# Second MLP stage of a transformer block: operand halves split over two slabs, combinations of the last chunk one per slab, x1 read back for two tiles

## The chip, the cores and the metric

One core of a Trainium2 chip runs the whole kernel in one launch. Times are device microseconds. The engines work side by side, each through its own queue in order: TensorE (PE, matrix products; PEld is its weight load), VectorE (DVE), ScalarE (ACT), GpSimd (POOL) and SyncE (SP), which here only issues DMAs. GpSimd and ScalarE issue DMAs too. An instruction whose input isn't there holds up everything behind it on its engine. The median of three runs before the change is 2258.95 us (2256.57 to 2261.75).

## The reference, cut to what matters

The block computes attention and retention, adds the result to x (this sum is called x1 here), and ends with an MLP. For 512 tokens of 2048 features in float32:

```python
x = x + rms_norm(mix, norm_mix_post[l])           # x1
h = rms_norm(x, norm_mlp_pre[l])
u = jnp.square(jax.nn.relu(h @ w_up[l]))          # first MLP stage: 512 x 8192
x = x + rms_norm(u @ w_down[l], norm_mlp_post[l]) # second MLP stage
```

`rms_norm(x, g)` is `x * rsqrt(mean(x*x) + eps) * g`, the mean over the 2048 features of a token. The change lies in the last line alone.

## The kernel before, in words

**Products.** Every float32 operand is split in two: a high half (a cast on ScalarE, `whi` for weights and `Hh` for the others) and a low half (the rest, a subtraction on VectorE, `wlo` and `Hl`). A product takes three matmuls: high by high, high by low, low by high (lines 154 to 156, helper `mm3`).

**Seven products instead of eight.** Both MLP stages cut their matrices in 2 x 2 blocks and form seven products of sums of blocks, after Winograd's form of Strassen's scheme. The products are numbered 0 to 6 and run in the order 0, 1, 2, 5, 4, 3, 6. Sums of weight blocks are made as the slabs come: by VectorE (line 949), for product 3 by an accumulating DMA from GpSimd (line 916). Sums of u blocks come ready-made from DRAM (`ud`).

**The second stage** (function `down`) goes through 8 chunks of the inner dimension (`c`), in each through two column halves of 1024 (`nb`), in each through the seven products: 112 phases. A phase is one product for two token tiles, two slabs of weights, 24 matmuls of 128x512. Per slab VectorE makes one `wlo` (line 929), and for products 2, 4 and 6 first a weight sum (line 949), which ScalarE's cast (line 953) needs. `Feed` holds three slabs in work.

After each phase `dn_done` adds the product to the sum `E[nb][p]` (line 1315; chunk 0 copies, line 1312). It is called at the next phase's first slab. In the last chunk it also forms the four result blocks from the seven sums: blocks 11 and 12 (token tiles 0 and 1; columns 0 to 511 and 512 to 1023 of the half), 21 and 22 (tiles 2 and 3). Before the change these combinations (lines 1319, 1323, 1324, 1327, 1335 to 1337) follow each other at once; `finished` squares a block on ScalarE with a running sum (line 1294), and `out_tile` makes the tile's root (line 1300, and a power on GpSimd in `inv_root`, line 161), scales by root and gain on VectorE (line 1304) and adds the result to `out` by an accumulating DMA from GpSimd (line 1305). `out` has held x1 since the start of the MLP. Tiles 2 and 3 wait for the very last product.

**The u operand.** `u_operand` fetches a product's u block from DRAM to a raw buffer through SyncE (line 1282) and splits it three slabs later: `split` issues the cast on ScalarE (line 143) and right behind it the subtraction on VectorE (line 144). Chunk 0 has two raw buffers (in `xh`), the others four (in rows 1 and 3 of `Y`); a fetch waits until the buffer's last subtraction is done. Weight slabs are fetched through SyncE as well (line 923).

**Order of the work.** The order of each engine's queue is the order in which this program emits instructions: per slab first `feed.slab()`, then `dn_done`, then what `later` has due (`later.add(n, work)` runs `work` n slabs on), then the matmuls.

Of the kernel before, what the change touches and what calls it, by code (L numbers as in the profile page):

```python
# [10 lines left out]
F32 = mybir.dt.float32  # L11
F32R = mybir.dt.float32r
AF = mybir.ActivationFunctionType
ALU = mybir.AluOpType
AX = mybir.AxisListType.X

P = 128
S = 512
NT = S // P
DM = 2048  # L20
# [92 lines left out]
def block_kernel(ctx: ExitStack, tc: tile.TileContext, x, norm_mix_pre, w_in, cmp_pe_k, cmp_w1_k, cmp_b1_k,  # L113
                 cmp_w2_k, cmp_pe_v, cmp_w1_v, cmp_b1_v, cmp_w2_v, t5_bias, w_out, norm_mix_post, norm_mlp_pre,
                 w_up, w_down, norm_mlp_post, c_rot, c_dec, c_hot, c_misc, out):
    nc = tc.nc
    x, out = x[0], out[0]
# [23 lines left out]
    def split(hi, lo, src):  # L141

        nc.scalar.copy(hi, src)  # L143
        nc.vector.tensor_sub(lo, src, hi.bitcast(F32))  # L144

    def rows_of(t):
        return slice(t * P, (t + 1) * P)

    def wide(g, c0, n):

        return bass.AP(tensor=g.tensor, offset=g.offset + c0, ap=[[0, P], [1, n]])

    def mm3(ps, ah, al, bh, bl, first, last):
        nc.tensor.matmul(ps, ah, bh, start=first, stop=False)  # L154
        nc.tensor.matmul(ps, ah, bl, start=False, stop=False)  # L155
        nc.tensor.matmul(ps, al, bh, start=False, stop=last)  # L156

    def inv_root(dst, ss, tmp, n, scale):

        nc.vector.tensor_scalar(tmp, ss, scale, EPS, op0=ALU.mult, op1=ALU.add)  # L160
        nc.gpsimd.tensor_tensor(dst, tmp, mhalf[:, :n], op=ALU.pow)
# [220 lines left out]
    for q in (2, 3):  # L382
        c = slice(q * 512, (q + 1) * 512)
# [19 lines left out]
    for n in range(4 * NT):  # L403
        t, q = n // 4, n % 4
# [142 lines left out]
    scale = DK ** -0.5  # L547
# [254 lines left out]
    fp = ctx.enter_context(tc.tile_pool(name="ffn", bufs=1, reuse_waits="tile"))  # L802
    Y = fp.tile([P, NT, DM], F32, name="Y")
    st = [fp.tile([P, 16], F32, name=f"st{t}") for t in range(NT)]
# [164 lines left out]
    class Later:  # L969
# [5 lines left out]
        def add(self, slabs, work):  # L975
            self.todo.append((self.at + slabs, work))
# [8 lines left out]
    later = Later()  # L985
# [119 lines left out]
    NCH = 8  # L1105
# [170 lines left out]
    ua = [tuple(H[:, c:c + SL] for H in (Hhf, Hlf)) for c in range(16, 16 + 7 * SL, SL)]  # L1276
    stage, stage0 = Ring(*(Y[:, t, c:c + SL] for t in (1, 3) for c in (0, SL))), Ring(xh[:, :SL], xh[:, SL:])

    def u_operand(c, p):

        r = (stage if c else stage0).take()
        nc.sync.dma_start(r.rearrange("p (b n) -> p b n", b=2), ud[p, 2 * c:2 * c + 2].rearrange("b p n -> p b n"))
        later.add(3, lambda: split(ua[p][0], ua[p][1], r))

    g4 = low[:, 4096:6144]

    def cols(nb, j):
        return slice(nb * 1024 + j * 512, nb * 1024 + (j + 1) * 512)

    def finished(nb, t0, j, v):  # L1290

        for t in (0, 1):
            jk = fp.tile([P, S], F32, name="jk", tag="jk")
            nc.scalar.activation(jk, v[:, t, :], AF.Square, accum_out=st[t0 + t][:, 2 * nb + j:2 * nb + j + 1])

    def out_tile(t, half):

        s = st[t]
        if half:
            nc.vector.reduce_sum(s[:, 5:6], s[:, 0:4], axis=AX)  # L1300
            inv_root(s[:, 7:8], s[:, 5:6], s[:, 6:7], 1, 1.0 / DM)
        for j in range(2):
            v = res[half, t // 2, j][:, t % 2, :]
            nc.vector.scalar_tensor_tensor(v, v, s[:, 7:8], g4[:, cols(half, j)], op0=ALU.mult, op1=ALU.mult)
            nc.gpsimd.dma_start(out[rows_of(t), cols(half, j)], v, accum_op=ALU.add)

    res = {}

    def dn_done(c, nb, p, ps):
        e = E[nb]  # L1310
        if c == 0:
            nc.scalar.copy(e[p], ps)
            return
        if c < NCH - 1 or p != 6:
            nc.vector.tensor_add(e[p], ps, e[p])  # L1315
        if c < NCH - 1:
            return
        if p == 1:
            nc.vector.tensor_add(e[1], e[1], e[0])
            res[nb, 0, 0] = e[1]  # L1320
            later.add(1, lambda: finished(nb, 0, 0, e[1]))
        elif p == 4:
            nc.vector.tensor_add(e[4], e[4], e[0])
            nc.vector.tensor_sub(e[2], e[2], e[4])

            def more():
                nc.vector.tensor_add(e[5], e[5], e[2])
                res[nb, 0, 1] = e[5]
                finished(nb, 0, 1, e[5])
                if nb:  # L1330
                    for n, (t, half) in enumerate(((0, 1), (0, 0), (1, 1), (1, 0))):
                        later.add(1 + n // 2, lambda t=t, half=half: out_tile(t, half))
            later.add(1, more)
        elif p == 3:
            nc.vector.tensor_add(e[4], e[4], e[3])
            nc.vector.tensor_add(e[6], e[6], e[4])
            nc.vector.tensor_sub(e[3], e[2], e[3])
            res[nb, 1, 1] = e[3]
            finished(nb, 2, 1, e[3])
        elif p == 6:  # L1340
            res[nb, 1, 0] = e[6]
            for t in (0, 1):
                nc.vector.tensor_add(e[6][:, t], ps[:, t], e[6][:, t])
                if nb:
                    jk = fp.tile([P, S], F32, name="jk", tag="jk")
                    nc.scalar.activation(jk, e[6][:, t], AF.Square, accum_out=st[2 + t][:, 2:3])
                    out_tile(2 + t, 1)
                    out_tile(2 + t, 0)
            if not nb:
                finished(nb, 2, 0, e[6])  # L1350

    sets2 = []

    def down():
        for i, ((_, c, nb), p, _) in enumerate(phases[nup:]):
            ps = pools[(nup + i) % len(pools)].tile([P, 2, S], F32, name="prod")
            final = nup + i == len(phases) - 1
            at = i % 7
            slabs = []
            for s in range(2):  # L1360
                slabs.append([v.rearrange("p (k n) -> p k n", k=2) for v in feed.slab()])
                if s == 0 and sets2:
                    dn_done(*sets2.pop())
                if s == 0 and i == 0:
                    up_done(*sets.pop())
                later.step()
                if s == 0 and i == 7:
                    nc.sync.dma_start(g4, wide(norm_mlp_post, 0, DM))
                if s == 1 and nb == 1 and c + 1 < NCH and at:
                    u_operand(c + 1, ORDER[at - 1])  # L1370
                if s == 1 and nb == 0 and at in ((0,) if c else (0, 1, 2)):
                    u_operand(c, 6 if c else ORDER[4 + at])
                if final and s == 0:
                    continue
                for t in range(2):
                    for s2 in range(2) if final else (s,):
                        for kk in range(2):
                            k = 2 * s2 + kk
                            uh, ul = (u.rearrange("p (k n) -> p k n", k=4) for u in ua[p])
                            mm3(ps[:, t, :], uh[:, k, rows_of(t)], ul[:, k, rows_of(t)], slabs[s2][0][:, kk, :],  # L1380
                                slabs[s2][1][:, kk, :], k == 0, k == 3)
            sets2.append((c, nb, p, ps))
        dn_done(*sets2.pop())


    for n, _ in enumerate(up(last, nup, pools, XA)):
        if n % 4 == 2 and n < 16:
            u_operand(0, ORDER[n // 4])
    sctx.close()
    accp = ctx.enter_context(tc.tile_pool(name="acc", bufs=1, reuse_waits="tile"))  # L1390
    Et = [accp.tile([P, SL], F32, name=f"acc{i}") for i in range(12)] + [xh[:, :SL], xh[:, SL:]]
    E = [[Et[nb * 7 + p].rearrange("p (t n) -> p t n", t=2) for p in range(7)] for nb in range(2)]
    down()
    while later.todo:
        later.step()
# [23 lines left out]
```

## Time and profile before

| | us |
|---|---|
| median of three runs | 2258.95 |
| profiled execution | 2263.74 |
| its span | 2261.9 |
| TensorE busy | 2175.6 (96%) |
| VectorE busy | 1563.7 (69%) |
| ScalarE busy | 986.9 (44%) |
| GpSimd busy | 129.1 (6%) |

The second stage's matmuls begin near 1595 us and end near 2233 us; the span ends at 2261.9 us. Busy shares are means over stages with different limits, so the stages are read one by one. Matmuls overlap in the trace: one lasts 0.39 us but starts 0.227 us after the one before it. A VectorE instruction on 1024 columns lasts 1.22 us, and the next starts 1.13 us after it. In a timeline a number of idle time in brackets, with an arrow, tells how long the engine stood and for whom.

### The profile page before, as it was taken

Reading aid. Unit: us, or ns where it says so; the run is one execution under the profiler, and the core shown is the slowest. Engines: PE = TensorE matmul, PEld = TensorE weight load, DVE = VectorE, ACT = ScalarE, POOL = GpSimd, SP = SyncE. Lnnn points to the kernel's source line nnn. Section 1 sums busy time; section 2 is a strip of 40 time slices with the busy share of each in tenths; the row PEclk is TensorE's granted clock in tenths of the full one; section 3 lists DMA queues with packets and bytes.
Section 4 is the critical chain, followed back from the end, with each engine's and each line's share of the span. In section 5 each row is a group of like instructions: output and inputs, shape, how many; then the busy total and the mean of one; then the engine's idle time right before and its main releaser. Section 6 shows DMA issues by size and latency. Waiting matters only on the chain.

```text
span 2261.9 us, 31774 instructions
## 1 busy us (share of the span) xinstructions
PE 2175.6 (96%) x12787; PEld 1919.0 (85%) x12787; DVE 1563.7 (69%) x1868; ACT 986.9 (44%) x1432; POOL 129.1 (6%) x147
## 2 busy tenths in 40 slices
PE   8999999999999999889999999999899999999994
PEld 7888878878787999889999999999778888888873
DVE  6223556554656623587777878787778998899897
ACT  5213343342232323564554555555654444444442
POOL 0000000000000000100000000000000000000002
PEclk9999999999999999999999999999999999999997
DMA  6543224322324334675876767666665656566655
GB/s 191 140 118 91 79 73 95 90 75 87 89 70 145 95 106 127 205 213 169 223 204 178 203 168 206 168 208 187 202 208 160 212 159 214 152 205 165 192 144 83
DMA packets 251989, 344.76 MB, mean 152 GB/s; under 512 B 14107, under 2 KB 163947, under 8 KB 251201
## 3 DMA queue, kind: packets, MB, share of 16 engines
q1 hardware_dynamic: 212000, 288.23, 39.4%
q0 software_dynamic: 29744, 42.96, 12.0%
q10 hardware_dynamic: 10098, 11.55, 1.5%
q8 instruction: 100, 1.64, 0.3%
q14 instruction: 47, 0.39, 0.1%
HBM read 300.95 MB, written 41.75 MB: 152 GB/s over the span
## 4 chain that ended last, share of the span: by engine, by line
PE 77%; DVE 12%; DMA 4%; ACT 3%; issue 3%; POOL 1%; SPq 0%; ACTq 0%; POOLq 0%; DVEq 0%
PE prod L155 13%; PE prod L156 13%; PE prod L154 13%; PE mm L154 11%; PE mm L156 10%; PE mm L155 10%; DVE wlo L929 4%; DMA Y<-in_w_up 2%; DVE Hl L144 2%; PE S L583 2%; ACT whi L953 1%; DVE low L949 1%; DVE Y L949 1%; DVE acc L1315 1%; DMA low<-in_w_up 1%
## 5 line engine op out<-in xcount | busy, mean ns | idle before, releaser
L953 ACT CAST whi<-Y 128x1024 fp32r<-128x1024 f32 x228 | 238.4, 1049 | 305.8 <-DVE Y L949 119.0
L155 PE MATMUL prod<-wlo,Hh 128*128 128x512 f32 x896 | 352.3, 393 | 18.3 <-DVE wlo L929 18.3
L156 PE MATMUL prod<-whi,Hl 128*128 128x512 f32 x896 | 349.0, 390 | 0.0
L154 PE MATMUL prod<-whi,Hh 128*128 128x512 f32 x896 | 348.7, 389 | 0.0
L953 ACT CAST whi<-low 128x1024 fp32r<-128x1024 f32 x214 | 224.3, 1052 | 282.2 <-DVE low L949 105.9
L144 DVE TENSOR_TENSOR wlo<-raw,whi 128x1024 fp32r<-128x1024 f32 (+4 forms) x152 | 168.6, 1113 | 255.9 <-ACT whi L143 255.4
L929 DVE TENSOR_TENSOR wlo<-Y,whi 128x1024 fp32r<-128x1024 f32 x228 | 277.6, 1222 | 61.6 <-ACT whi L953 59.9
L929 DVE TENSOR_TENSOR wlo<-low,whi 128x1024 fp32r<-128x1024 f32 x214 | 260.8, 1222 | 54.4 <-ACT whi L953 52.7
L156 PE MATMUL prod<-Hh,wlo 128*128 128x256 f32 x1024 | 286.2, 279 | 11.2 <-DVE wlo L929 11.2
L154 PE MATMUL prod<-Hh,whi 128*128 128x256 f32 x1024 | 285.7, 279 | 5.1 <-DVE Y L824 5.1
L155 PE MATMUL prod<-Hl,whi 128*128 128x256 f32 x1024 | 284.7, 278 | 0.0
L143 ACT CAST whi<-raw 128x1024 fp32r<-128x1024 f32 (+4 forms) x152 | 145.4, 960 | 302.5 <-PE mm L155 147.9
L154 PE MATMUL mm<-whi,Hh 128*128 128x416 f32 (+4 forms) x704 | 263.3, 374 | 0.5 <-ACT Hh L143 0.4
L156 PE MATMUL mm<-whi,Hl 128*128 128x416 f32 (+4 forms) x704 | 248.6, 353 | 0.6 <-DVE Hl L144 0.5
L155 PE MATMUL mm<-wlo,Hh 128*128 128x416 f32 (+4 forms) x704 | 248.1, 352 | 0.0
L155 PEld LDWEIGHTS prod<-wlo,Hh 128*128 128x128 f32 x896 | 168.1, 188 | 65.5 <-DVE wlo L929 31.0
L156 PE MATMUL prod<-sx,wlo 128*128 128x256 f32 x768 | 215.1, 280 | 8.1 <-DVE wlo L929 8.1
L154 PE MATMUL prod<-sx,whi 128*128 128x256 f32 x768 | 214.7, 280 | 0.5 <-ACT whi L953 0.5
L154 PE MATMUL mm<-Hh,whi 128*128 128x512 f32 x512 | 214.7, 419 | 0.1
L155 PE MATMUL prod<-sx,whi 128*128 128x256 f32 x768 | 214.5, 279 | 0.0
L156 PEld LDWEIGHTS prod<-Hh,wlo 128*128 128x128 f32 x1024 | 194.3, 190 | 13.6 <-DVE wlo L929 13.4
L156 PE MATMUL mm<-Hh,wlo 128*128 128x512 f32 x512 | 200.5, 392 | 0.0
(289 smaller groups left out, 3970.4 us busy)
## 6 DMA issues: line engine op xcount, KB each, us to landing
raw<-in_w_in SPq DMA_DIRECT2D x160, 256.0 KB, 3.1
low<-in_w_up SPq DMA_DIRECT2D x38, 1024.0 KB, 6.2
Y<-in_w_up SPq DMA_DIRECT2D x32, 1024.0 KB, 6.1
low<-in_w_down SPq DMA_DIRECT2D x32, 1024.0 KB, 5.2
Y<-in_w_down SPq DMA_DIRECT2D x32, 1024.0 KB, 5.2
Y<-ud SPq DMA_DIRECT2D x49, 512.0 KB, 8.4
ud<-Y SPq DMA_DIRECT2D x73, 256.0 KB, 4.7
raw<-in_w_out SPq DMA_DIRECT2D x32, 416.0 KB, 3.5
```

What stands on the lines that cost most here:

```text
L143: nc.scalar.copy(hi, src)
L144: nc.vector.tensor_sub(lo, src, hi.bitcast(F32))
L154: nc.tensor.matmul(ps, ah, bh, start=first, stop=False)
L155: nc.tensor.matmul(ps, ah, bl, start=False, stop=False)
L156: nc.tensor.matmul(ps, al, bh, start=False, stop=last)
L583: nc.tensor.matmul(sps[:, :c + L], QT[g][:, h, qs], k, start=True, stop=True)
L929: nc.vector.tensor_sub(lo, src, hi.bitcast(F32))
L949: nc.vector.tensor_add(to, to, by)
L953: nc.scalar.copy(hi, src)
L1315: nc.vector.tensor_add(e[p], ps, e[p])
```

## The change

- The u operand's cast stays three slabs behind its fetch; the subtraction is issued one slab later, four behind.
- In the last chunk the combinations are put into two lists, `vec` and `act`, and `spare()` takes at most one entry from each per slab. The combinations are written as single additions and subtractions, nine per column half instead of seven. The gain is multiplied in on VectorE block by block (`gained`), where it was part of the last scaling before.
- Tiles 0 and 1: ScalarE scales by the root (`out_first`), and GpSimd's accumulating DMA adds to `out` as before.
- Tiles 2 and 3: x1 is read back from `out` into rows 1 and 3 of `Y` during the last chunk's first half; VectorE scales and adds x1 in one instruction (`out_last`), and SyncE writes the result by a plain DMA.
- In the second column half, products 4 and 3 first empty both lists and then do what the next block needs at once.

```diff
--- before.py
+++ after.py
@@ -1280,74 +1280,134 @@
 
         r = (stage if c else stage0).take()
         nc.sync.dma_start(r.rearrange("p (b n) -> p b n", b=2), ud[p, 2 * c:2 * c + 2].rearrange("b p n -> p b n"))
-        later.add(3, lambda: split(ua[p][0], ua[p][1], r))
+        later.add(3, lambda: nc.scalar.copy(ua[p][0], r))
+        later.add(4, lambda: nc.vector.tensor_sub(ua[p][1], r, ua[p][0].bitcast(F32)))
 
     g4 = low[:, 4096:6144]
 
     def cols(nb, j):
         return slice(nb * 1024 + j * 512, nb * 1024 + (j + 1) * 512)
 
-    def finished(nb, t0, j, v):
-
-        for t in (0, 1):
-            jk = fp.tile([P, S], F32, name="jk", tag="jk")
-            nc.scalar.activation(jk, v[:, t, :], AF.Square, accum_out=st[t0 + t][:, 2 * nb + j:2 * nb + j + 1])
-
-    def out_tile(t, half):
-
+
+    vec, act = [], []
+
+    def spare():
+        for todo in (act, vec):
+            if todo:
+                todo.pop(0)()
+
+    res = {}
+
+    def square(nb, q, t, v):
+
+        jk = fp.tile([P, S], F32, name="jk", tag="jk")
+        nc.scalar.activation(jk, v, AF.Square, accum_out=st[t][:, 2 * nb + q % 10 - 1:2 * nb + q % 10])
+
+    def gained(nb, q, v, ts):
+
+        g = g4[:, None, cols(nb, q % 10 - 1)]
+        nc.vector.tensor_tensor(v[:, ts], v[:, ts], g.to_broadcast([P, ts.stop - ts.start, S]), op=ALU.mult)
+
+    def there(nb, q, v):
+
+        res[nb, q] = v
+
+        def squares():
+            for t in (0, 1):
+                square(nb, q, q // 10 * 2 - 2 + t, v[:, t])
+            vec.append(lambda: gained(nb, q, v, slice(0, 2)))
+        act.append(squares)
+
+    def root(t):
         s = st[t]
-        if half:
-            nc.vector.reduce_sum(s[:, 5:6], s[:, 0:4], axis=AX)
-            inv_root(s[:, 7:8], s[:, 5:6], s[:, 6:7], 1, 1.0 / DM)
-        for j in range(2):
-            v = res[half, t // 2, j][:, t % 2, :]
-            nc.vector.scalar_tensor_tensor(v, v, s[:, 7:8], g4[:, cols(half, j)], op0=ALU.mult, op1=ALU.mult)
-            nc.gpsimd.dma_start(out[rows_of(t), cols(half, j)], v, accum_op=ALU.add)
-
-    res = {}
+        nc.vector.reduce_sum(s[:, 5:6], s[:, 0:4], axis=AX)
+        inv_root(s[:, 7:8], s[:, 5:6], s[:, 6:7], 1, 1.0 / DM)
+
+    def quarters(t):
+        for nb in range(2):
+            for j in range(2):
+                yield res[nb, t // 2 * 10 + 11 + j][:, t % 2], cols(nb, j)
+
+    def out_first(t):
+
+        for v, c in quarters(t):
+            nc.scalar.activation(v, v, AF.Copy, scale=st[t][:, 7:8])
+            nc.gpsimd.dma_start(out[rows_of(t), c], v, accum_op=ALU.add)
+
+    x1b = {2: Y[:, 1, :], 3: Y[:, 3, :]}
+
+    def out_last(t):
+
+        for v, c in quarters(t):
+            nc.vector.scalar_tensor_tensor(v, v, st[t][:, 7:8], x1b[t][:, c], op0=ALU.mult, op1=ALU.add)
+            nc.sync.dma_start(out[rows_of(t), c], v)
 
     def dn_done(c, nb, p, ps):
         e = E[nb]
         if c == 0:
             nc.scalar.copy(e[p], ps)
             return
-        if c < NCH - 1 or p != 6:
-            nc.vector.tensor_add(e[p], ps, e[p])
+        if c == NCH - 1 and p == 6 and nb:
+            for t in (0, 1):
+                ts = slice(t, t + 1)
+                nc.vector.tensor_add(e[6][:, t], ps[:, t], e[6][:, t])
+                square(1, 21, 2 + t, e[6][:, t])
+                gained(1, 21, e[6], ts)
+                root(2 + t)
+                out_last(2 + t)
+            return
+        nc.vector.tensor_add(e[p], ps, e[p])
         if c < NCH - 1:
             return
+
+        def op(f, to, by):
+            vec.append(lambda: f(e[to], e[to], e[by]))
+
+        add, sub = nc.vector.tensor_add, nc.vector.tensor_sub
         if p == 1:
-            nc.vector.tensor_add(e[1], e[1], e[0])
-            res[nb, 0, 0] = e[1]
-            later.add(1, lambda: finished(nb, 0, 0, e[1]))
+            op(add, 1, 0)
+            vec.append(lambda: there(nb, 11, e[1]))
+        elif p == 2:
+            op(sub, 2, 0)
+        elif p == 5:
+            op(add, 5, 2)
+            op(add, 6, 0)
+        elif p == 4 and not nb:
+            op(sub, 5, 4)
+            vec.append(lambda: there(nb, 12, e[5]))
+            op(sub, 2, 4)
+            op(add, 6, 4)
         elif p == 4:
-            nc.vector.tensor_add(e[4], e[4], e[0])
-            nc.vector.tensor_sub(e[2], e[2], e[4])
-
-            def more():
-                nc.vector.tensor_add(e[5], e[5], e[2])
-                res[nb, 0, 1] = e[5]
-                finished(nb, 0, 1, e[5])
-                if nb:
-                    for n, (t, half) in enumerate(((0, 1), (0, 0), (1, 1), (1, 0))):
-                        later.add(1 + n // 2, lambda t=t, half=half: out_tile(t, half))
-            later.add(1, more)
+            while vec or act:
+                spare()
+            sub(e[5], e[5], e[4])
+            res[1, 12] = e[5]
+            for t in (0, 1):
+                square(1, 12, t, e[5][:, t])
+            op(sub, 2, 4)
+
+            def roots():
+                gained(1, 12, e[5], slice(0, 2))
+                for t in (0, 1):
+                    root(t)
+                    act.append(lambda t=t: out_first(t))
+            vec.append(roots)
+            op(add, 6, 4)
+        elif p == 3 and not nb:
+            op(sub, 2, 3)
+            vec.append(lambda: there(nb, 22, e[2]))
+            op(add, 6, 3)
         elif p == 3:
-            nc.vector.tensor_add(e[4], e[4], e[3])
-            nc.vector.tensor_add(e[6], e[6], e[4])
-            nc.vector.tensor_sub(e[3], e[2], e[3])
-            res[nb, 1, 1] = e[3]
-            finished(nb, 2, 1, e[3])
+            while vec or act:
+                spare()
+            sub(e[2], e[2], e[3])
+            res[1, 22], res[1, 21] = e[2], e[6]
+            for t in (0, 1):
+                square(1, 22, 2 + t, e[2][:, t])
+            add(e[6], e[6], e[3])
+            gained(1, 22, e[2], slice(0, 2))
         elif p == 6:
-            res[nb, 1, 0] = e[6]
-            for t in (0, 1):
-                nc.vector.tensor_add(e[6][:, t], ps[:, t], e[6][:, t])
-                if nb:
-                    jk = fp.tile([P, S], F32, name="jk", tag="jk")
-                    nc.scalar.activation(jk, e[6][:, t], AF.Square, accum_out=st[2 + t][:, 2:3])
-                    out_tile(2 + t, 1)
-                    out_tile(2 + t, 0)
-            if not nb:
-                finished(nb, 2, 0, e[6])
+            vec.append(lambda: there(nb, 21, e[6]))
 
     sets2 = []
 
@@ -1364,6 +1424,9 @@
                 if s == 0 and i == 0:
                     up_done(*sets.pop())
                 later.step()
+                spare()
+                if c == NCH - 1 and nb == 0 and at in (4, 5) and s:
+                    nc.sync.dma_start(x1b[at - 2], out[rows_of(at - 2), :])
                 if s == 0 and i == 7:
                     nc.sync.dma_start(g4, wide(norm_mlp_post, 0, DM))
                 if s == 1 and nb == 1 and c + 1 < NCH and at:
```

## Rows read from the trace of the kernel before

**Rows 1.** Stretches; from:to, length, busy us (instructions) by engine, granted clock, DMA share, GB/s.
```profile
1740.00:1817.50 77.50, 76.99 (x337) 62.78 (x336) 70.75 (x61) 35.72 (x36) 4.73 (x4) 1.00 0.61 183
2128.00:2205.00 77.00, 72.89 (x315) 58.05 (x314) 73.68 (x65) 38.34 (x49) 4.73 (x4) 1.00 0.52 157
```

**Rows 2.** Waits of TensorE and VectorE, 1595 to 1700; us in total, times, longest.
```profile
PE prod L155 <- DVE wlo L929: 10.0, 7, 2.4
...
DVE Hl L144 <- ACT Hh L143: 20.3, 10, 3.4
```

**Rows 3.** Timeline of VectorE and TensorE, 1607 to 1612; start, duration, instruction, idle before.
```profile
1608.32 1.23 DVE L144 TENSOR_TENSOR Hl<-xh,Hh 128x1024 fp32r<-128x1024 f32 x1 [1.89 <-ACT Hh L143]
...
1610.60 2.48 DVE L929 TENSOR_TENSOR wlo<-low,whi 128x1024 fp32r<-128x1024 f32 x2
...
1611.87 0.50 PE L155 MATMUL prod<-wlo,Hh 128*128 128x512 f32 x1 [2.38 <-DVE wlo L929]
```

**Rows 4.** Chain that ended last: the same cast, five chunks apart; start, us.
```profile
1738.60 1.05 ACT whi L953
...
2126.50 1.06 ACT whi L953
```

**Rows 5.** Timeline of TensorE in the last chunk: 142 matmul starts apart.
```profile
2192.72 0.39 PE L156 MATMUL prod<-whi,Hl 128*128 128x512 f32 x1
...
2224.93 0.39 PE L154 MATMUL prod<-whi,Hh 128*128 128x512 f32 x1
```

**Rows 6.** Timeline of VectorE in the last chunk.
```profile
2176.57 1.22 DVE L929 TENSOR_TENSOR wlo<-low,whi 128x1024 fp32r<-128x1024 f32 x1
2177.70 1.22 DVE L1315 TENSOR_TENSOR acc<-prod,acc 128x1024 f32<-128x1024 f32 x1
2178.96 1.23 DVE L1323 TENSOR_TENSOR acc<-acc,acc 128x1024 f32<-128x1024 f32 x1
```

**Rows 7.** Waits of SyncE's DMA queue, second MLP stage.
```profile
SPq L1282 <- DVE Hl L144: 19.1, 5, 5.9
```

**Rows 8.** DMA issues; out<-in, queue, count, KB each, median us to landing.
```profile
low<-in_w_down SPq DMA_DIRECT2D x32, 1024.0 KB, 5.2
...
ud<-Y SPq DMA_DIRECT2D x73, 256.0 KB, 4.7
...
xh<-ud SPq DMA_DIRECT2D x7, 512.0 KB, 4.5
```

**Rows 9.** Timeline of VectorE at the end.
```profile
2229.41 0.75 DVE L1304 SCALAR_TENSOR_TENSOR acc<-acc,st,low 128x512 f32<-128x512 f32 x1 [0.75 <-POOL st L161]
2230.08 0.74 DVE L1304 SCALAR_TENSOR_TENSOR xh<-xh,st,low 128x512 f32<-128x512 f32 x1
...
2247.41 0.16 DVE L1300 TENSOR_REDUCE st<-st 128x1 f32<-128x4 f32 x1 [0.85 <-ACT jk L1346]
...
2249.18 2.07 DVE L1304 SCALAR_TENSOR_TENSOR acc<-acc,st,low 128x512 f32<-128x512 f32 x3
```

**Rows 10.** Waits of VectorE, 2128 to 2233.
```profile
DVE wlo L929 <- ACT whi L953: 2.0, 4, 1.4
```

**Rows 11.** Timeline of GpSimd at the end.
```profile
2228.81 0.56 POOL L161 TENSOR_TENSOR st<-st,misc 128x1 f32<-128x1 f32 x1 [24.75 <-DVE st L160]
...
2249.56 0.88 POOL L1305 DMA_DIRECT2D out<-xh  x1 [1.08 <-DVE xh L1304]
2250.22 2.86 POOL L1305 DMA_DIRECT2D out<-acc  x3
```

**Rows 12.** Timeline of ScalarE: one square of 512 columns and the reading of its sum.
```profile
2206.66 0.63 ACT L1294 ACTIVATE jk<-acc 128x512 f32<-128x512 f32 x1 [2.19 <-DVE acc L1319]
2207.19 0.19 ACT L1294 ACTIVATION_READ_ACCUMULATOR jk<-acc 128x1 f32 x1
```

**Rows 13.** Stretches at the end, columns as in the first group.
```profile
2236.00:2238.00 2.00, 0.00 (x0) 0.00 (x0) 1.21 (x4) 0.94 (x3) 0.57 (x1) 0.50 0.95 161
...
2258.00:2260.00 2.00, 0.00 (x0) 0.00 (x0) 0.00 (x0) 0.00 (x0) 0.00 (x0) 0.50 0.26 46
```

## The prediction

> **What bounds the kernel now.** I read the table of stretches first, then the waits, then the timeline of single engines, last the end of the chain. The second MLP stage is eight chunks of 14 products. In a middle chunk TensorE has 76.99 of 77.50 us busy and VectorE 70.75 [rows 1]. So TensorE is the bound there, and VectorE, which makes the low half of every weight slab, follows at 91%. In the last chunk VectorE is at 73.68 of 77.00 us and TensorE falls to 72.89 [rows 1]: the two have changed places.
>
> Two kinds of lost time are to be seen. At the stage's start TensorE waits seven times, 10.0 us together, for a low half from VectorE, while VectorE itself waits ten times, 20.3 us together, for the cast of a u operand on ScalarE [rows 2]. One case in full: VectorE stands 1.89 us before L144 at 1608.32, because that subtraction is queued right behind the cast it reads; the weight's low halves behind it start at 1610.60; TensorE gets one at 1611.87, after 2.38 us of waiting [rows 3]. The other kind is the end, where VectorE does add after add to the last result and the transfers follow it.
>
> **Part one: the operand's low half one slab later.** Removed is VectorE's wait for the cast. No instruction is added: cast and subtraction are the same, and the subtraction now stands behind a slab's worth of other VectorE work, when the cast has long ended. What it gives is read from TensorE.
>
> First two chunks: the seven stalls are 10.0 us [rows 2]. The bounds are 0 (the products' combinations of the first MLP stage still run there, and could make VectorE late by themselves) and 10.0. I take 9.5, near the upper end: the case in rows 3 loses 1.89 on VectorE and 2.38 on TensorE, and VectorE's 20.3 us are twice what TensorE lost.
>
> Chunks three to seven: the same weight cast stands at 1738.60 and at 2126.50 [rows 4], five chunks apart, 77.58 us each. A matmul costs (2224.93 - 2192.72) / 142 = 0.2268 us [rows 5], so 336 of them cost 76.2. The loss is 1.38 us a chunk, 6.9 in five. I take all of it: in the half chunk with six operands VectorE has 14 low halves, 6 weight sums, 7 accumulations and 6 operand halves, 33 x 1.13 = 37.3 us [rows 6] beside 38.1 us of matmuls, so without waits it keeps up. The first part of chunk eight, before its combinations, loses the same once: 1.4. Bounds for both together 0 and 8.3.
>
> Part one: 9.5 + 6.9 + 1.4 = **17.8 us less**.
>
> What is late next: the raw buffer is freed a slab later (12 matmuls, 2.72 us). In the first chunk its ring has two views, and SyncE already waited there five times, 19.1 us, for such a subtraction before fetching the next operand [rows 7]. I take 0 for it: the fetch lands in 4.5 us [rows 8] and its cast comes three slabs, 8.2 us, after the issue. Without that cover it costs up to 5 x 2.72 = 13.6 us, since weight loads stand behind it on SyncE. Later chunks have four views.
>
> **Part two: the last chunk.** From its first product on VectorE sets the end in both versions, so I count VectorE. Each column half had 7 combinations; it has 9, and multiplications with the gain: 4 in the first half, 3 and two half-sized ones in the second. That is 6 + 5 = 11 instructions more, at 1.13 us (2176.57 to 2177.70) [rows 6]: +12.5. Where a combination takes what the instruction before it wrote, it starts 1.26 us later instead of 1.13 (2177.70 to 2178.96) [rows 6]; 12 of the old ones do, hardly any of the new: -1.5. The scalings of 512 columns fall from 16 to 8, at 0.67 us (2229.41 to 2230.08) [rows 9]: -5.4. VectorE no longer waits for GpSimd's power for tiles 0 and 1, 0.75 us each [rows 9]: -1.5. Its four waits for weight casts in this chunk, 2.0 us [rows 10], get filled by the one combination per slab: -2.0 (0 if not). The two half-sized gains lie in the 0.85 us in which VectorE waits for a square anyway [rows 9]: 0.
>
> One wait is new. On ScalarE the squares of the last but one block stand behind eight scalings of tiles 0 and 1, and the gain on VectorE waits for those squares, with the last two tiles behind it. Power 0.56 [rows 11], eight at 0.63 [rows 12] and two squares of 0.63 and 0.19 make 7.2 us; VectorE has four instructions for that time, 4.8 us: +2.4 (bounds 0 and 7.2).
>
> Sum on VectorE: 12.5 - 1.5 - 5.4 - 1.5 - 2.0 + 2.4 = +4.5.
>
> TensorE's stalls in this chunk grow with it, and cost nothing themselves, as the last two half accumulations find VectorE busy. In the longest the clock may fall: after the last matmuls, near 2233, TensorE stands idle and the granted clock from 2236 on is 0.50, the 1.2 GHz level [rows 13]. The final 24 matmuls would then take 5.4 us more, within the 7 us by which VectorE is behind them.
>
> Behind the last scaling: it ended at 2249.18 + 2.07 = 2251.25 [rows 9], the last accumulating transfer about 2258.5 (the stretch from 2258 has 0.26 of DMA share, against 0.95 at 2236) [rows 13]: 7.2 us. The new last write is a plain one of the same 256 KB on SyncE: 0.5 to issue and 4.7 to land, the row of such a write [rows 8]: 5.2, so -2.0. Bounds: 4.7 alone, and the old 7.2.
>
> GpSimd's queue: tile 2's power stands behind eight DMA issues, of which four took from 2249.56 to 2253.08, 0.88 us each [rows 11]: 7.0, done some 2 us before VectorE wants the power. The x1 reads are two issues on SyncE, needed 50 us later: 0, with the rival below.
>
> Two powers now run beside VectorE, where the old ones had it idle for 0.75 us [rows 9]; no row shows both at work. The Trainium skill (SBUF — State Buffer, "Who interferes with whom") says that a VectorE instruction with two SBUF inputs and a GpSimd instruction that reads SBUF block one another for the whole instruction. By that rule each power would wait for up to one 1.22 us add; the sum would then be 2.4 us worse.
>
> Part two: 4.5 - 2.0 = **2.5 us more**. Together -17.8 + 2.5 = **-15.3**.
>
> The profiled execution took 2263.7 us (span 2261.9 and 1.8 around it), 4.8 above the median of 2258.95; 2263.7 - 15.3 = 2248.4. I take the difference over to the median: **2243.6**.
>
> **Rivals.**
> *The first two chunks keep their stalls*, because the first MLP stage's leftover VectorE work makes them. For: the stage's first stall is at its border. Against: VectorE's waits exceed TensorE's [rows 2]. Then -6.9 - 1.4 + 2.5 = -5.8: 2253.2.
> *The x1 reads hold up the last weight loads* on SyncE. For: one read is issued right ahead of the last two loads. Each megabyte takes 5.2 us to land [rows 8], two 10.4: -15.3 + 10.4 = -4.9: 2254.0. Against: the DMA share there is 0.52 [rows 1]. The Trainium skill (DMA: Bandwidth & Descriptors, "Issuing engines are not separate DMA queues") says that transfers of all issuing engines share the same 16 DMA engines and interleave, so the choice of queue would not shield the loads; no row here has such a read.
> *The change does not do what it says*: the subtraction still finds its cast unfinished, as ScalarE is the late one. Then only part two is left: +2.5, 2261.4. Against: ScalarE is busy 35.72 of 77.50 us [rows 1].
> *Slower: SyncE's queue in the first chunk.* Each of five operand fetches waits a slab longer, the weight loads behind it come late by 13.6 us in all, and TensorE loses that in place of the 9.5 gained: +13.6 - 8.3 + 2.5 = +7.8: 2266.8. It decides once a fetch comes over 3.7 us late (8.2 less the 4.5 of its landing) [rows 8].
>
> **How the numbers follow.** Forecast 0.72, with its own range 2237 to 2250 (6.5 either way: 4.8 if the new ScalarE wait is at its upper end, 2.0 from the last write, and part of the stalls). Kept stalls 0.10, x1 reads 0.06, no effect 0.06, slower 0.06. The range goes from 2236 to 2256, which takes in the first two rivals. A measurement of this kernel tells 0.2%, 4.5 us, from no change: faster is below 2254.4, slower above 2263.5. Faster: 0.72, most of kept stalls (0.06) and half of the x1 case (0.04): 0.82. Same: the rest of these and most of "no effect": 0.11. Slower 0.07.
>
> **What would show it.** VectorE's waits for the operand casts should be gone, and TensorE's seven stalls with them; five middle chunks should span 381 us instead of 387.9; in the last chunk TensorE should wait more than before and VectorE have no idle time until the squares behind the eight scalings; the last SyncE write should land about 5 us after the last scaling. Middle chunks that still take 77.6 us, or SyncE waiting longer ahead of weight loads, would prove it wrong.

## The result, and the profile after

The changed kernel takes 2236.57 us (median of five runs, 2230.31 to 2248.12) against 2258.95: a ratio of 0.990 with an interval of 0.987 to 0.993, some 22 us less. That lies at the fast edge of the range that was forecast, 0.6 us inside its bound of 2236, and 7.0 us below the forecast itself, 2243.6. The profiled execution also took 2236.57 us, its span 2234.8.

The profiled executions of the kernels here reach the second stage between 1586.5 and 1604.8 us, although no variant touches what comes before it; so lengths are compared from the second stage's first 128x512 matmul to the span's end. This length and its parts are differences of start and end times in the timelines. "First chunk" ends with VectorE's first accumulation of chunk two, "last chunk" runs from the first accumulation of chunk eight to the end of VectorE's last instruction, and "behind" is what follows to the span's end.

| us | first chunk | second | a middle chunk | last chunk | behind | stage | against before |
|---|---|---|---|---|---|---|---|
| before | 94.69 | 77.54 | 77.58 | 95.50 | 10.65 | 666.3 | |
| after | 83.55 | 75.49 | 76.16 | 100.78 | 3.45 | 644.1 | -22.3 |

First the waits of the changed kernel (total us, times, longest): TensorE's and VectorE's at the stage's start, 1595 to 1700, which answer to [rows 2], then SyncE's from 1580 to the end, which answer to [rows 7].

```profile
PE prod L155 <- DVE wlo L929: 0.5, 1, 0.5
...
DVE wlo L929 <- ACT whi L953: 13.2, 14, 1.5
...
DVE Hl L1284 <- ACT Hh L1283: 4.3, 7, 1.3
...
SPq L1282 <- DVE Hl L1284: 18.6, 5, 5.6
```

TensorE's seven stalls of 10.0 us are one of 0.5. VectorE still stands idle, but now mostly for weight casts, ahead of the low halves that have just become possible: it is early, not late. SyncE waits no longer for operand buffers than before (18.6 us in 5 against 19.1 in 5).

VectorE's timeline at the place that answers to [rows 3] (start, duration, instruction):

```profile
1600.81 1.22 DVE L929 TENSOR_TENSOR wlo<-low,whi 128x1024 fp32r<-128x1024 f32 x1
1601.94 1.22 DVE L1284 TENSOR_TENSOR Hl<-xh,Hh 128x1024 fp32r<-128x1024 f32 x1
1603.08 1.22 DVE L929 TENSOR_TENSOR wlo<-low,whi 128x1024 fp32r<-128x1024 f32 x1
```

The operand's low half stands between two weight halves at the bare step of 1.13 us. In [rows 3] VectorE stood 1.89 us ahead of the same instruction.

Two stretches, a middle chunk and the last, columns as in [rows 1], then two accumulations five chunks apart, which answer to [rows 4]:

```profile
1740.00:1817.50 77.50, 77.50 (x343) 64.17 (x343) 71.84 (x63) 36.82 (x36) 4.73 (x4) 1.00 0.62 184
2105.00:2182.00 77.00, 73.22 (x318) 58.99 (x317) 76.69 (x68) 37.05 (x46) 4.73 (x4) 1.00 0.60 186
```

```profile
1749.77 1.22 DVE L1359 TENSOR_TENSOR acc<-prod,acc 128x1024 f32<-128x1024 f32 x1
...
2130.57 1.22 DVE L1359 TENSOR_TENSOR acc<-prod,acc 128x1024 f32<-128x1024 f32 x1
```

TensorE has no gap left in the middle chunk, and five chunks take 380.8 us (before 387.9). In the stretch of the last chunk VectorE is busy 76.69 of 77 us.

The last chunk: waits of TensorE and VectorE, TensorE's longest stall, and the stretches in it and behind it.

```profile
PE prod L155 <- DVE wlo L929: 11.0, 6, 6.0
...
DVE acc L1309 <- ACT jk L1304: 2.4, 1, 2.4
```

```profile
2208.64 0.80 PE L155 MATMUL prod<-wlo,Hh 128*128 128x512 f32 x1 [5.97 <-DVE wlo L929]
```

```profile
2206.00:2208.00 2.00, 0.00 (x0) 0.00 (x0) 2.00 (x3) 1.19 (x3) 0.00 (x0) 0.50 0.00 0
2212.00:2214.00 2.00, 2.00 (x10) 1.62 (x10) 2.00 (x3) 2.00 (x4) 1.43 (x3) 1.00 0.00 0
2230.00:2232.00 2.00, 0.00 (x0) 0.00 (x0) 1.35 (x3) 0.00 (x0) 0.00 (x0) 0.50 0.92 339
```

TensorE stands 5.97 us for one low half that is queued behind combinations; the granted clock falls to 0.50 (1.2 GHz) in that stall, the first matmul after it takes 0.80 us, and by 2212 the clock is 1.00 again. The 23 matmuls from there on take 1.6 us more than at 0.227 us each. This costs nothing: TensorE ends at 2215.67, and VectorE comes to the last half accumulations at 2219.54.

Last, the two kinds of write (2205 to 2235): for each kind of DMA queue its packets, MB and the time that they took, as a share of the 16 DMA engines; then count, KB each, median us from issue to landing. They answer to [rows 8] and the end in [rows 9]. The accumulating writes go through GpSimd's queue (software), the plain ones through SyncE's (hardware):

```profile
q0 software_dynamic: 1152, 2.10, 46.2%
q1 hardware_dynamic: 1152, 2.10, 18.8%
...
out<-acc POOLq DMA_DIRECT2D x6, 256.0 KB, 7.8
out<-acc SPq DMA_DIRECT2D x6, 256.0 KB, 2.5
```

For the same 2.10 MB the accumulating writes occupy the DMA engines 2.5 times as long. The plain writes' median of 2.5 us hides two cases. Those of tile 2, issued while accumulating ones are still under way, land in some 5.1 us (three of four are in the trace), the first of them 0.5 us after the last accumulating one (2228.68 and 2228.19). Those of tile 3, issued later, land in 2.3 to 2.6 us. The last transfer starts right behind VectorE's end at 2231.35, and the span ends 3.45 us after that end.

### The profile page after: what moved, and what is told of

It reads as the page before. It is cut to its first block, busy times and chain, and to the rows that moved or that the text cites. A ratio compares the mean times of both kernels' runs of the same rounds, so it can differ in the third digit from the quotient of the medians.

```text
span 2234.8 us, 31796 instructions
## 1 busy us (share of the span) xinstructions
PE 2168.3 (97%) x12787; PEld 1920.1 (86%) x12787; DVE 1568.4 (70%) x1872; ACT 993.1 (44%) x1440; POOL 121.9 (5%) x139
## 4 chain that ended last, share of the span: by engine, by line
PE 84%; DVE 8%; DMA 4%; ACT 2%; issue 2%; SPq 0%; POOL 0%; DVEq 0%; ACTq 0%; POOLq 0%
PE prod L156 15%; PE prod L154 15%; PE prod L155 15%; PE mm L154 11%; PE mm L156 10%; PE mm L155 10%; DVE wlo L929 2%; DMA Y<-in_w_up 2%; PE S L583 2%; DMA low<-in_w_up 1%; DVE Y L949 1%; PE S L706 1%; PE PT L646 1%; PE oT L741 1%; PE oT L501 1%
```

## The experiments

**The two parts, each alone.** The first is the kernel before with the subtraction one slab later, the second the changed kernel without it:

```diff
-        later.add(3, lambda: split(ua[p][0], ua[p][1], r))
+        later.add(3, lambda: nc.scalar.copy(ua[p][0], r))
+        later.add(4, lambda: nc.vector.tensor_sub(ua[p][1], r, ua[p][0].bitcast(F32)))
```

> The kernel before with part one alone (cast three slabs behind the fetch, subtraction four). Theory: the trace after shows 1.5 us won at the stage's border, 11.1 in the first chunk and 9.2 in the next six, and all of it belongs to this edit and reaches the end, as VectorE's work behind it is the old one: 21.8 us less, about 2237 us, middle chunks at 76.2 us, no wait of VectorE for an operand's cast in them. Rival: part of the 21.8 comes from part two or from run to run; then about 2245 or more.

> The changed kernel with cast and subtraction issued together again, three slabs behind the fetch: part two alone. Theory: VectorE's last chunk is 5.3 us longer and the end behind its last scaling 7.2 us shorter, so 1.9 us less, about 2257 us, with the old stalls at the stage's start. Rival, the forecast's own sum: 2.5 us more, about 2261.5 us.

| us | first chunk | a middle chunk | last chunk | behind | stage | against before |
|---|---|---|---|---|---|---|
| first part alone | 83.56 | 76.16 | 95.36 | 9.98 | 645.2 | -21.2 |
| second part alone | 94.71 | 77.58 | 100.82 | 3.41 | 664.4 | -1.9 |

Medians: 2236.99 us (ratio 0.991, 0.988 to 0.994) and 2259.5 (1.000, 0.997 to 1.003). The first part carries nearly the whole gain, as its theory had it. The second, too, came as its theory had it, 1.9 us less; the rival, the forecast's own 2.5 us more, fell. The second part makes the last chunk 5.3 us longer and what follows it 7.2 shorter. The waits of the second part's kernel at the start, 1588 to 1693, show the old pair, operand subtraction for its cast and TensorE for the weight's low half:

```profile
DVE Hl L144 <- ACT Hh L143: 17.9, 9, 3.4
...
PE prod L155 <- DVE wlo L929: 10.1, 7, 2.4
```

**Is it the distance from the fetch, or the adjacency of cast and subtraction?** Both are moved a slab, still one behind the other; the rest is the kernel before.

```diff
-        later.add(3, lambda: split(ua[p][0], ua[p][1], r))
+        later.add(4, lambda: split(ua[p][0], ua[p][1], r))
```

> The kernel before with cast and subtraction both four slabs behind the fetch, still one behind the other. Theory: what costs is that the subtraction stands in VectorE's queue right behind its own cast, so nothing is won by moving both: 2257 to 2261 us, VectorE still waits some 20 us for casts between the stage's start and its second chunk, middle chunks still 77.5 us. Rival: the subtraction only had to leave the slab in which much else is due; then 2240 to 2248 us.

The stage took 682.0 us, 15.7 more than before (median 2277.94, ratio 1.008, 1.005 to 1.012): first chunk 91.05, a middle chunk 80.23. This kernel differs from the first part alone only in the cast, which comes a slab later and so stands right ahead of its reader again; that costs 36.8 us of the stage (682.0 against 645.2). The adjacency is the cause, as the theory had it, but that the kernel would then be as slow as before was wrong both ways: a middle chunk is 2.65 us longer than before, the first chunk 3.6 us shorter. Waits of 1740 to 2128, and one case:

```profile
DVE Hl L144 <- ACT Hh L143: 22.4, 23, 1.6
...
PE prod L155 <- DVE wlo L929: 9.0, 25, 0.4
```

```profile
1823.53 1.22 DVE L929 TENSOR_TENSOR wlo<-low,whi 128x1024 fp32r<-128x1024 f32 x1
...
1825.75 1.23 DVE L144 TENSOR_TENSOR Hl<-Y,Hh 128x1024 fp32r<-128x1024 f32 x1 [1.00 <-ACT Hh L143]
```

```profile
1824.68 1.04 ACT L143 CAST Hh<-Y 128x1024 fp32r<-128x1024 f32 x1
```

VectorE is done with the weight half at 1824.75 and stands 1.00 us until the cast that began at 1824.68 is over. In the same stretch the kernel before shows this line:

```profile
DVE Hl L144 <- ACT Hh L143: 7.7, 10, 0.8
```

One slab later the pair falls into a slab without an accumulation, so VectorE has nothing to do while the cast runs. In the middle chunks the distance from the fetch is not at fault; what counts is how much other VectorE work stands between a cast and its reader. At the stage's start moving the pair did help: TensorE's stalls fell from 10.0 us to 4.4, though only setting the two apart ended them (0.5). Why the later pair helps there is open.

**Why is the end shorter?** All four tiles are written by accumulating DMAs, without the x1 reads. The last instruction multiplies by a tile of ones, so that VectorE's work keeps its length.

```diff
-            nc.vector.scalar_tensor_tensor(v, v, st[t][:, 7:8], x1b[t][:, c], op0=ALU.mult, op1=ALU.add)
-            nc.sync.dma_start(out[rows_of(t), c], v)
+            nc.vector.scalar_tensor_tensor(v, v, st[t][:, 7:8], E[1][0][:, 0], op0=ALU.mult, op1=ALU.mult)
+            nc.gpsimd.dma_start(out[rows_of(t), c], v, accum_op=ALU.add)
...
+            nc.gpsimd.memset(e[0], 1.0)
...
-                if c == NCH - 1 and nb == 0 and at in (4, 5) and s:
-                    nc.sync.dma_start(x1b[at - 2], out[rows_of(at - 2), :])
```

> The changed kernel, but tiles 2 and 3 are scaled on VectorE by an instruction of the same form (it multiplies by a tile of ones that GpSimd sets early in the last chunk) and added to the output by GpSimd's accumulating DMA, as tiles 0 and 1; the two x1 reads are gone. Theory: the 7.2 us won behind the last scaling come from the plain write, so the end behind it grows from 3.4 us to 9 to 11 us, and the kernel takes about 2243 us, 6 to 7 more than the changed one; the last chunk is otherwise as long. Rival: the end is short because fewer transfers are left by then; then it stays within 2 us of the changed kernel.

Last chunk 100.83 us (after: 100.78), behind it 10.1 (after: 3.45), median 2240.13 (0.992, 0.989 to 0.995). So the x1 reads cost nothing, and the kind of the last writes, with the queue that goes with it, is worth 6.7 us. The two are not told apart: no run has a plain write in GpSimd's queue. Its writes (2205 to 2239), and a stretch at the end:

```profile
out<-acc POOLq DMA_DIRECT2D x12, 256.0 KB, 6.7
```

```profile
2234.00:2236.00 2.00, 0.00 (x0) 0.00 (x0) 0.00 (x0) 0.00 (x0) 0.00 (x0) 0.50 1.07 194
```

The DMA engines are as full as with plain writes (share 1.07 against 0.92 at 2230 in the changed kernel), but move 194 GB/s instead of 339: an accumulating write occupies them longer for the same bytes. The last tile's four land 1.3 us apart, from 2233.38 to 2237.22, the last of them 8.0 us after its issue.

**Can GpSimd take the gains off VectorE?** Five multiplications of 1.13 us would leave it.

```diff
-            vec.append(lambda: gained(nb, q, v, slice(0, 2)))
+            g = g4[:, None, cols(nb, q % 10 - 1)]
+            vec.append(lambda: nc.gpsimd.tensor_tensor(v, v, g.to_broadcast([P, 2, S]), op=ALU.mult))
```

> The changed kernel, with the gain of five of the seven full blocks multiplied in on GpSimd, idle until then, instead of VectorE. Theory: the last chunk is bound by VectorE's count of instructions, so five fewer at 1.13 us take 5.7 us off its last chunk (100.8 to about 95), with no more than 1 us given back: about 2231 us. Rival, the Trainium skill's rule (SBUF — State Buffer, 'Who interferes with whom') that VectorE with two SBUF inputs and GpSimd reading SBUF block each other for a whole instruction: VectorE's additions beside the five multiplications then last up to a GpSimd instruction longer, and the last chunk is not shorter than 100 us.

The last chunk grew to 108.52 us, 7.7 more than in the changed kernel (median 2247.0 against 2269.57 for the kernel before beside it, 0.993, 0.990 to 0.996). VectorE and GpSimd at two multiplications:

```profile
2146.09 1.23 DVE L1365 TENSOR_TENSOR acc<-acc,acc 128x1024 f32<-128x1024 f32 x1
2147.23 3.39 DVE L949 TENSOR_TENSOR Y<-Y 128x1024 f32<-128x1024 f32 x1
...
2180.57 10.45 DVE L929 TENSOR_TENSOR wlo<-Y,whi 128x1024 fp32r<-128x1024 f32 x2
```

```profile
2146.41 3.13 POOL L1319 TENSOR_TENSOR acc<-acc,low 128x1024 f32<-128x1024 f32 x1 [10.12 <-ACT jk L1304]
...
2182.46 7.47 POOL L1319 TENSOR_TENSOR acc<-acc,low 128x1024 f32<-128x1024 f32 x3
```

A VectorE weight sum beside a multiplication on GpSimd takes 3.39 us instead of 1.22. Of the two subtractions, merged here in one line, the first takes 1.22 us and the second 9.20: it ends 1.1 us after the last of three multiplications. A third such case takes 3.43 us. Together VectorE loses 12.4 us this way and saves 5 x 1.13 = 5.7. The theory fell, and its rival held.

**The order at the end.** The new wait of 2.4 us for the squares is to be filled: the squares of the last but one block go on ScalarE between the four scalings of tile 0 and the four of tile 1, and the last block's work goes step by step for both tiles.

```diff
-            while vec or act:
-                spare()
+            while vec:
+                vec.pop(0)()
+            act.pop(0)()
             sub(e[2], e[2], e[3])
...
+            act.pop(0)()
...
-                gained(1, 21, e[6], ts)
+            for t in (0, 1):
+                gained(1, 21, e[6], slice(t, t + 1))
                 root(2 + t)
+            for t in (0, 1):
                 out_last(2 + t)
```

> The changed kernel with the same instructions at the end in another order: the squares of the last but one block stand behind four of the eight scalings, not eight, and the two last half blocks go through add, square, gain and root side by side instead of one after the other. Theory: the 2.4 us wait of VectorE for those squares, two waits of 0.85 for a square and one of 0.75 for a power are what it costs; 3.5 to 4.5 us off the last chunk (100.8 to about 97), about 2233 us. Rival: the transfers of tile 0 and 1 set the end, then the tail behind the last scaling grows by as much.

The last chunk fell to 96.39 us, 4.4 less, but what follows it rose from 3.45 to 7.32; the stage is 0.6 us shorter (643.5). The median, 2234.25 (0.986, 0.982 to 0.990), cannot be told from the changed kernel's. Its writes (2195 to 2232):

```profile
out<-acc POOLq DMA_DIRECT2D x6, 256.0 KB, 7.0
out<-acc SPq DMA_DIRECT2D x6, 256.0 KB, 5.9
```

With VectorE done earlier all plain writes, the last tile's too, are issued while accumulating ones are on their way. The first, issued at 2218.06, lands at 2224.74, 0.2 us after the last accumulating one, and the median is 5.9 us instead of 2.5. Most of the time gained was lost to this, nearly as the rival had it.

**Both together, and the changed kernel once more beside it.**

> The two edits before this one together. Theory: both shorten the same queue of VectorE, so they add up until TensorE's last matmul is waited for: last chunk 90 to 93 us, about 2227 us. Rival: TensorE's six-microsecond wait before its last product leaves it as the bound, and the sum is no better than the better of the two.

> The changed kernel once more, beside the three others on one chip. Every theory: 2232 to 2241 us, middle chunks 76.16 us, last chunk 100.8 us, 3.4 us behind the last scaling.

Both edits: last chunk 104.01 us where 90 to 93 were expected, behind it 7.34, stage 650.8, median 2242.76 (0.990, 0.986 to 0.994). GpSimd's cost stays, and the order's gain comes off it: 100.8 + 7.7 - 4.4 = 104.1. The changed kernel again: 100.81, 3.43 and 644.1, all within 0.1 us of the first profile (median 2234.47; 0.986, 0.982 to 0.989).

**Seven combinations instead of nine.** In the last chunk's first half product 4 is first added to product 0, and the sum is then used twice, as in the kernel before; still one combination per slab. The second of the two kernels adds the order at the end.

```diff
...
         elif p == 4 and not nb:
-            op(sub, 5, 4)
+            op(add, 4, 0)
+            op(sub, 2, 4)
+            op(add, 5, 2)
             vec.append(lambda: there(nb, 12, e[5]))
-            op(sub, 2, 4)
-            op(add, 6, 4)
...
         elif p == 3 and not nb:
+            op(add, 4, 3)
             op(sub, 2, 3)
             vec.append(lambda: there(nb, 22, e[2]))
-            op(add, 6, 3)
+            op(add, 6, 4)
...
```

> The changed kernel, with the first column half of the last chunk combined in seven instructions as before the change (the second half in nine). Theory: VectorE's count sets the last chunk, so two instructions fewer take 2.3 us off it (100.8 to 98.5) and nothing is given back behind the last scaling (3.4 us): 2 us less than the changed kernel. Rival: TensorE's stalls in that half come back, because three combinations now fall due at one product, and the last chunk stays at 100 us or more.

> The one before with the end reordered as in the run where four scalings stood ahead of the squares. There VectorE won 4.4 us and the tail behind it gave back 3.9. Theory: the accumulating transfers of tiles 0 and 1 start when VectorE reaches their roots, so they start 2.3 us earlier here too; last chunk about 94 us, tail 7.3 us, together 101.5 against 104.2 for the changed kernel: 2.5 us less. Rival: the last writes land no earlier than in the run before this one, as the sum stays at 103.5 or more.

The first: last chunk 98.64 us, 2.1 less than in the changed kernel, behind it 3.39, stage 641.5. The second: 94.23 and 7.25, stage 641.3. So two combinations less are worth two steps of VectorE, and the second kernel's last chunk and tail sum to the 101.5 us expected. These are the shortest stages of all, 24.8 and 25.0 us under the kernel before. Their medians (2244.71, 0.990, 0.986 to 0.994; and 2239.11, 0.989, 0.985 to 0.993) do not separate them from the changed kernel, as 2.7 us is far below the 18 by which the start of the second stage varies.

## Why the prediction was right, and which terms were mis-sized

| term, us | forecast | measured |
|---|---|---|
| part one, up to the first accumulation of chunk eight | -16.4 | -20.3 |
| part one, in chunk eight | -1.4 | -0.1 (first part alone) |
| part two, VectorE's last chunk | +4.5 | +5.3 |
| part two, behind the last scaling | -2.0 | -7.2 |
| sum | -15.3 | -22.3 |

The mechanism of part one held: the waits went as described, and the time with them. Sizes were off, above all behind the last scaling. Part two has the wrong sign: forecast 2.5 us more, measured 1.9 less. The misses add to 7.0 us, the two largest (3.9 in part one, 5.2 behind the last scaling) on the same side, so the result falls just outside the 2237 to 2250 that the main forecast was given 0.72 for. That it still falls inside the outer range, by 0.6 us, is in part luck: the bounds of the terms reach only 3.4 us to the fast side (2.4 in the new wait, 0.5 in the stalls, 0.5 in the last write), and the five runs lie between 2230.31 and 2248.12.

*The cause of the stalls* is shown by three kernels: subtraction apart from its cast (0.5 us left), both unmoved beside the new last chunk (10.1 us in 7), both moved together (4.4 us at the start, and every later chunk longer than before).

*First two chunks, -9.5:* the first chunk gave 11.1 and the second 2.05. The listed stalls fell by 9.5, as said (10.0 to 0.5). What was left out is the steady loss of 1.4 us a chunk, most of it in gaps too short to be listed (the list shows 2.5 us in 10 for the five middle chunks): it was counted for chunks three to seven, and the first two should have it as well. 9.5 + 2 x 1.4 = 12.3, of the 13.2 measured; the last 0.9 is not assigned to an instruction.

*Five middle chunks, -6.9:* 387.9 to 380.8. Right.

*Chunk eight, -1.4:* did not come. With the first part alone the last chunk took 95.36 us against 95.50: VectorE sets the end there from the first product on, as the prediction itself said one paragraph later, and time that TensorE gains doesn't count.

*VectorE's last chunk, +4.5:* +5.3. The new wait behind the eight scalings was sized well (2.38 us for 2.4 forecast). The four waits for weight casts did get filled: none is left. GpSimd's eight issues took 7.1 us, from 2213.00 to 2220.08, and were done 2.1 us before tile 2's power (forecast 7.0 and 2). The term that failed is the 0 for the two half-sized gains. They do not lie in the wait for the square but behind it:

```profile
2219.54 0.68 DVE L1353 TENSOR_TENSOR xh<-prod,xh 128x512 f32<-128x512 f32 x1
2221.07 0.69 DVE L1309 TENSOR_TENSOR xh<-xh,low 128x512 f32<-128x512 f32 x1 [0.85 <-ACT jk L1304]
2221.68 0.15 DVE L1323 TENSOR_REDUCE st<-st 128x1 f32<-128x4 f32 x1
```

The gain is multiplied into the very block that the square reads, so VectorE stands the whole 0.85 us and then needs 0.61 more, twice: +1.2. Four combinations still follow at once what they read, 1.25 us after it: +0.5. Other terms take 0.9 of this back and are not assigned. The slow clock behind TensorE's longest stall cost 1.6 us where 5.4 were feared, and nothing at the end.

*Behind the last scaling, -2.0:* the largest miss, 5.2 us, in three parts. The old end was misread: the last accumulating write was issued at 2251.54 and landed 8.5 us later, 8.8 behind the last scaling, where a DMA share near 2258 had been read as 7.2. The new landing was taken from a row of writes amid the traffic of a busy stage, 4.7 us and 0.5 to issue [rows 8]; with the accumulating writes out of the way it took 2.5. And from the last landing to the span's end 1.8 us pass in the kernel before and 0.9 in the changed one, which was left out. The experiment with accumulating writes puts 6.7 of the 7.2 us on the kind of write and its queue. The order at the end shows the condition: beside accumulating writes the plain one takes 5.9.

*The rivals.* Kept stalls in the first two chunks and a change without effect fell with the waits. The x1 reads cost nothing. The slower rival, SyncE's queue in the first chunk, fell too: SyncE waited 18.6 us for operand buffers, no longer than before, although each buffer is freed a slab later. VectorE, no longer held up, reached the freeing subtraction earlier: the last of these waits ended 16.2 us into the stage, before the change 20.3. In the chances, half of the x1 rival's 0.06 is 0.03, not 0.04, so "faster" should have had 0.81.

*The powers beside VectorE* were weighed with a rule of the Trainium skill at 2.4 us. The trace shows nothing of it: each of the first two powers lasted 0.54 us on GpSimd, but the VectorE instruction beside them was an accumulation (L1359) with only one input in SBUF, so the rule was not put to the test there. The experiment with the gains on GpSimd put it to the test, and there it held.

## What to carry to other kernels

Where an engine reads what another makes from the same input, put a slab's worth of its other work between the two in its queue: the wait costs little on that engine itself, but everything queued behind it comes late for the engine that sets the pace. When such a loss is read from a trace, measure the period too and not only the listed stalls, in every stage where the pattern runs. And where the last write follows the last result, price it as it will find the DMA engines at that moment, plain rather than accumulating, with earlier transfers out of its way.

## What the runs showed of the hardware

GpSimd's multiplication of 128x1024 holds up VectorE's work on two SBUF inputs: 3.39 us instead of 1.22 for VectorE beside 3.13 on GpSimd. This is the rule of the Trainium skill (SBUF — State Buffer, "Who interferes with whom"): a VectorE instruction with two SBUF inputs contends with a GpSimd instruction that reads SBUF. The traces agree as to VectorE; whether GpSimd was held up as well is not shown.

Accumulating writes of 256 KB, through GpSimd's queue and several at a time, took 6.7 to 7.8 us to land at the end (medians); a plain one through SyncE's took 2.5 with none of them under way, at 194 and 339 GB/s with the DMA engines about full. In all eight traces that have both kinds the first plain write was issued 4.5 to 6.6 us before the last accumulating one landed, and landed 0.2 to 0.8 us after it.

TensorE has two paces at the same granted clock. The same stretch of the first MLP stage in two executions whose code is the same there, the kernel with both edits and the changed one:

```profile
1300.00:1400.00 100.00, 100.00 (x852) 100.00 (x851) 77.32 (x77) 52.28 (x64) 5.08 (x4) 1.00 0.62 172
```

```profile
1300.00:1400.00 100.00, 100.00 (x884) 100.00 (x884) 80.05 (x81) 56.08 (x70) 5.09 (x4) 1.00 0.65 186
```

It is busy throughout in both, at a granted clock of 1.00, and does 852 matmuls in one and 884 in the other (median step 0.118 and 0.113 us). What sets the pace stays open.
